# Logits from 64-row products in neighbouring PSUM banks, and wide gate and up products, in a four-layer decoder trunk

## The chip, the cores and the metric

The kernel runs on one core of a Trainium2 chip. The metric is the device time of one execution in microseconds (us). Before the change the median of three runs is 1354.68 us (1350.62 to 1355.57).

## What is computed

Four decoder layers over 256 positions of width 1024, all in float32. A layer is a token mixer, a cross-attention of four heads into 256 memory tokens, one output projection, and a SwiGLU feed-forward block; each of the two sub-layers ends in `x = LayerNorm(alpha * x + sublayer(x))`. Layers 0 and 3 select 64 keys for every query with an indexer and attend to them, layer 1 is a dilated attention of three groups, layer 2 attends causally. All have heads of 64 columns.

```
logits = einsum('bhqd,bhkd->bhqk', q, k) * 64 ** -0.5
p      = softmax(where(mask, logits, -inf))
mix    = einsum('bhqk,bhkd->bhqd', p, v)
x = layer_norm(ALPHA * x + concat(mix, memory_attention) @ w_out)
g, u = split(x @ w_gate_up, 2)            # 1024 -> 2 x 2816
x = layer_norm(ALPHA * x + (silu(g) * u) @ w_down)
```

## The kernel before, in words

**Two parts.** TensorE (PE) multiplies in the type float32r, which keeps fewer bits than float32, so each operand is held in two parts: a high part (`wh`, `xh`, `fth`, `pbh`, ...), a cast that ScalarE (ACT) makes, and a low part (`wl`, `xl`, ...), the difference, which VectorE (DVE) or GpSimd (POOL) makes. `mm3` (L253) is one product in three: high by high, and the two mixed ones (L256 to L258).

**Weights.** They arrive as 128x1024 float32 halves through the SP queue into four `raw` buffers, are cast into one of six pairs of buffers (L214 on ACT, L230 on DVE or L228 on POOL), and are freed by the product that reads them last.

**Products.** `t_mode` (L291) makes a transposed result: for each of two column groups and each of eight 128-row pieces it issues one `mm3` with the weights standing and 256 columns of x moving, and both groups lie in one PSUM bank. The feed-forward block makes 22 such gate and up pieces per layer, the first two in another mode; each is finished by `t_task` (L1055): SiLU on ACT out of PSUM (L1057), a product with the up half on DVE (L1059), a cast (L1061) and a difference (L1063). `down` (L306) uses them with 512 moving columns.

**Mixers.** For a pair of heads, `a_mode` makes q and k for 128 positions in a bank, `rotated` (L462) copies them out (L465), rotates them on DVE (L457 to L460), and transposes them on PE into another bank (L473). `qk_task` (L582) writes q and k from there: `q_parts` puts the high part of a head in one half of the partitions and the low part in the other, `k_parts` and `k_cross` (two more ACT copies, L492 and L493) put each head's k in both halves, so that `logits` (L495) needs one 128-row product per head for 128 keys (L500) and two for 256 keys (L504). `softmax` works in the bank of the logits; `turned` (L548) transposes the probabilities into another bank (L555), from which `split` makes the two parts `pah`/`pal` (128 keys) or `pbh`/`pbl` (256 keys): all casts on ACT (L265), then all differences on DVE (L270). `attend` (L562) multiplies them by the values, and `diag_out` splits the result into `fth`/`ftl`, 64 rows at a time.

**Order.** PE runs in the order in which the Python code issues its instructions. Attention tasks are generators that go on by one step at every `tick`, between pieces of products; a task that finds no free buffer waits a tick. The other engines' order is made from priorities, and each engine works through its own in order.

**Banks.** The eight PSUM banks are a `Slots` list (L86): `pop` takes the bank that was given back longest ago, `put` appends. A bank is given back when its last reader is issued, not when it has run; the next product into that bank waits for the reader. The feed-forward block keeps four banks as accumulators.

```
    def put(self, x):
        self.free.append(x)

    def pop(self):
        return self.free.pop(0)
```

Of the kernel before, what the change touches and what calls it, by code (L numbers as in the profile page):

```python
# [18 lines left out]
S = 256  # L19
# [63 lines left out]
    return out  # L83


class Slots:  # L86
    def __init__(self, items):
        self.free = list(items)
# [24 lines left out]
class K:  # L113
    def __init__(self, tc, io, ctx):
        self.tc, self.nc, self.io = tc, tc.nc, io
        pool = lambda n: ctx.enter_context(tc.tile_pool(name=n, bufs=1))
        self.sb = pool("sb")
        self.pp = ctx.enter_context(tc.tile_pool(name="ps", bufs=1, space=bass.MemoryType.PSUM))

        ctx.enter_context(tc.manual_schedule(engines={mybir.EngineType.PE}))  # L120
        self.stalls = {}
        self.tasks = []
        T = self.t
        pair = lambda shp, tag, n: Slots([(T(shp, F32R, f"{tag}h{i}"), T(shp, F32R, f"{tag}l{i}")) for i in range(n)])
        one = lambda shp, tag, n, dt=F32: Slots([T(shp, dt, f"{tag}{i}") for i in range(n)])
        self.banks = Slots([self.pp.tile([128, 512], F32, name=f"bank{i}") for i in range(8)])
        self.raws = one([128, HALF], "raw", NR)
        self.cvs = pair([128, HALF], "w", NB)
        self.nats = one([128, 256], "nat", 3)
        self.qs = one([128, 2, 128], "q", 4, F32R)  # L130
        self.qms = one([128, 2, S], "qm", 2, F32R)
        self.es = {128: one([128, 2, 128], "e", 3), 256: one([128, 2, 256], "E", 3)}
        self.pTs = {1: pair([128, 1, 2, 128], "pa", 2), 2: pair([128, 2, 2, 128], "pb", 2)}
        self.vs = pair([128, 2, 256], "v", 3)
        self.fts = pair([128, S], "ft", 8)
        self.sils = one([128, S], "sil", 3)
        self.kks = one([128, 2, 2, S], "k", NKB, F32R)
# [3 lines left out]
        self.mk = [T([128, 2, 2, S], F32R, f"mk{i}") for i in range(2)]  # L141
# [149 lines left out]
    def t_mode(self, xT, key):  # L291
        b = self.take(self.banks, "bank")
        p = b.rearrange("p (c t) -> p c t", c=2)
        for c in range(2):
            for k in range(8):
                w = self.half(key, k // 4)
                cs = slice((k % 4) * 256 + c * 128, (k % 4) * 256 + c * 128 + 128)
                self.mm3(p[:, c], (w[0][:, cs], w[1][:, cs]), (xT[0][:, k], xT[1][:, k]), k == 0, k == 7)
                if k % 4 == 3:
                    if c:  # L300
                        self.free_half(key, k // 4)
                    if not (c and k == 7):
                        self.tick()
        return b, p

    def down(self, accs, what, l, kb, tb, ft, first):  # L306
        ts = slice(tb * 128, tb * 128 + 128)
# [168 lines left out]

    def q_parts(self, dst, src, scale=None):

        lo, hi = slice(0, 64), slice(64, 128)
        return [(dst[lo, 0], dst[hi, 0], src[lo], scale), (dst[hi, 1], dst[lo, 1], src[hi], scale)]

    def k_parts(self, dst, src):

        d = dst.rearrange("p h a t -> p a h t")
        n = src.shape[1]
        return d[:, 0], d[:, 1], src[:, None, :].to_broadcast([128, 2, n]), None

    def k_cross(self, dst):  # L490
        lo, hi = slice(0, 64), slice(64, 128)
# [3 lines left out]
    def logits(self, b, q, ks, nk):  # L495

        mm = self.nc.tensor.matmul
        for h in range(2):
            if nk == 128:
                mm(b[:, h * 256:h * 256 + 256].rearrange("p (a s) -> p a s", a=2), lhsT=q[:, h], rhs=ks[h][:, :, 0:128],  # L500
                   start=True, stop=True)
            else:
                for part in range(2):
                    mm(b[:, h * 256:h * 256 + 256], lhsT=q[:, h], rhs=ks[h][:, part], start=part == 0, stop=part == 1)  # L504

    def pair_logits(self, b, q, kb, nk):
        self.logits(b, q, [kb[:, h] for h in range(2)], nk)

    def read_logits(self, b, nk):
        if nk == 128:  # L510
            L = b.rearrange("p (h a s) -> p h a s", h=2, a=2)
            return L[:, :, 0], L[:, :, 1]
        return (b.rearrange("p (h s) -> p h s", h=2),)

    def exps(self, L, e, mn, sm, mask=None, dst=None):

# [14 lines left out]
    def softmax(self, nk, product, mask=None):  # L531

        nc = self.nc
        b = yield from self.tk(self.banks)
        st = yield from self.tk(self.sts)
        e = yield from self.tk(self.es[nk])
        product(b)
        L = self.read_logits(b, nk)
        self.exps(L, e, st[:, 0:2], st[:, 2:4], mask)
        yield W_EXP  # L540
        nc.vector.reciprocal(st[:, 4:6], st[:, 2:4])
        nc.vector.tensor_tensor(e, L[0], st[:, 4:6, None].to_broadcast([128, 2, nk]), op=OP.mult)
        self.banks.put(b)
        self.sts.put(st)
        yield W_NORM
        return e
# [45 lines left out]
    def head_task(self, bank, tb, kb, q, flags, masks, vs, vi, col, mix, kbi):  # L592
# [3 lines left out]
        nk = 128 * (tb + 1)  # L596

        def product(b):
            self.pair_logits(b, q[tb], kb, nk)
# [24 lines left out]

    def mk_piece(self, l):
        b, p = self.t_mode(self.memT, ("mk", l, 0))
        self.split(*(self.k_parts(self.mk[pp], p[:, pp]) for pp in range(2)))
        for pp in range(2):
            self.k_cross(self.mk[pp])
        self.banks.put(b)  # L630
        self.tick()

# [7 lines left out]
    def qm_piece(self, l):  # L640
        b, p = self.t_mode(self.xT, ("qm", l, 0))
        qm = [self.take(self.qms, "qm") for _ in range(2)]
        self.split(*(x for pp in range(2) for x in self.q_parts(qm[pp], p[:, pp], SCALE)))
        self.banks.put(b)
        self.tick()
        return qm
# [1 line left out]
    def mem_task(self, qm, pp, tb, mix):  # L648
        ts = slice(tb * 128, tb * 128 + 128)

        def product(b):
            self.pair_logits(b, qm[pp][:, :, ts], self.mk[pp], S)
# [12 lines left out]
    def ki_task(self, bank, tb, kb, wi, kg, kbb, flags):  # L665
# [21 lines left out]
        self.split((kb[:, 0, 0, tb * 128:tb * 128 + 128], kb[:, 0, 1, tb * 128:tb * 128 + 128], b[:, 0:128], None))  # L687
        self.banks.put(b)
        yield W_K
        flags.add(("k", tb))  # L690
# [1 line left out]
    def qi_task(self, bank, tb, c, qi, mix):  # L692
        b, p = yield from self.rotated(bank, tb)
        for i in range(2):
            qi[tb, 2 * c + i] = mix[2 + 2 * c + i][tb].rearrange("p (h t) -> p h t", h=2)
        self.split(*(x for i in range(2) for x in self.q_parts(qi[tb, 2 * c + i], p[:, i])))
        self.banks.put(b)
        yield W_K
        qi[tb, "ready", c] = True
# [1 line left out]
    def select_task(self, tb, qi, kb, wi, flags, masks):  # L701
# [6 lines left out]
        for pr in range(4):  # L708
            while (tb, "ready", pr // 2) not in qi:
                yield 1  # L710
            b = yield from self.tk(self.banks)
            rl = yield from self.tk(self.es[nk])
            self.logits(b, qi[tb, pr], [kb[:, 0]] * 2, nk)
            L = self.read_logits(b, nk)
            r = L[0]
            if len(L) == 2:
# [148 lines left out]
    def dil_task(self, bank, tb, kb, q, flags, g, parts, jp):  # L865
# [8 lines left out]
        b = yield from self.tk(self.banks)  # L874
        e = yield from self.tk(self.es[nk])
        self.pair_logits(b, q[tb], kb, nk)
        self.qs.put(q[tb])
        flags.add(("l", tb))
        if ("l", 0) in flags and ("l", 1) in flags:
# [155 lines left out]
    def ffn(self, l, ts):  # L1035
# [38 lines left out]
        self.ln_params("ln2", l)  # L1074

        def gu(i):
            b, p = self.t_mode(self.xT, ("gu", l, i))
            fts[i] = self.take(self.fts, "ft")
            gut[i, 0] = gut[i, 1] = self.spawn(t_task(i, b, p))
            self.tick()  # L1080

        def ready(kb, tb):
# [118 lines left out]
```

## Time and profile before

| | |
|---|---|
| median of three runs | 1354.68 us (1350.62 to 1355.57) |
| the profiled execution's own time | 1351.82 us |
| its span | 1350.0 us |
| PE busy | 1287.3 us (95%) |
| PE weight loads busy | 1212.5 us (90%) |
| DVE, ACT, POOL busy | 897.5, 762.9, 316.4 us (66, 57, 23%) |
| granted TensorE clock, mean | 0.983 |
| DMA | 225.65 MB, 167 GB/s over the span |

The span is that of the instructions; the time also holds what lies around them. Matmuls are pipelined: a row's mean duration is longer than the distance between the starts of two that follow each other, and the distance is what a product costs a busy PE. Idle time of an engine that is not the bottleneck costs nothing.

### The profile page before, as it was taken

How to read it: one execution, taken by the hardware profiler on the slowest of the kernel's cores; microseconds unless marked ns; L12 is line 12 of the kernel's file. 1: busy time of each engine (PE TensorE's matmuls, PEld its weight loads, DVE VectorE, ACT ScalarE, POOL GpSimd, SP SyncE). 2: the span in 40 equal slices, each digit the busy share in tenths (PEclk: the TensorE clock that was granted, in tenths of full speed). 3: DMA queues.
4: the chain of work that ended last, by engine and by line, in shares of the span. 5: the costliest groups of instructions: out<-in, count | busy, mean ns of one | idle time of the engine just before them, and what ended most of it. 6: DMA issues, size and time to landing. Idle time of an engine off the chain costs nothing. (4 is left out here: it accounts for less than half of the span.)

```text
span 1350.0 us, 24249 instructions
## 1 busy us (share of the span) xinstructions
PE 1287.3 (95%) x9186; PEld 1212.5 (90%) x9186; DVE 897.5 (66%) x1940; ACT 762.9 (57%) x1512; POOL 316.4 (23%) x277
## 2 busy tenths in 40 slices
PE   6889899999999789999999999999999899999997
PEld 5879799999999779999989989999999898899996
DVE  7887775555578886555567877555568997655555
ACT  5668754444469745444447986444445897544441
POOL 3434440000045343000034444000014533300000
PEclk9989999999999889999999999999999999999999
DMA  8443356556564136565545345666546333655551
GB/s 300 126 149 110 110 180 199 187 188 184 170 203 150 70 103 240 185 189 180 183 155 180 133 141 169 206 185 188 186 138 218 127 125 126 203 188 188 187 176 59
DMA packets 63190, 225.65 MB, mean 167 GB/s; under 512 B 7776, under 2 KB 7776, under 8 KB 63072
## 3 DMA queue, kind: packets, MB, share of 16 engines
q1 hardware_dynamic: 62784, 224.10, 50.2%
q8 instruction: 72, 1.18, 0.4%
q14 instruction: 46, 0.38, 0.1%
q10 hardware_dynamic: 288, 0.00, 0.0%
HBM read 223.02 MB, written 1.05 MB: 166 GB/s over the span
## 5 line engine op out<-in xcount | busy, mean ns | idle before, releaser
L214 ACT CAST wh<-raw 128x1024 fp32r<-128x1024 f32 (+1 forms) x402 | 420.8, 1048 | 318.6 <-PE bank L257 177.2
L230 DVE TENSOR_TENSOR wl<-raw,wh 128x1024 fp32r<-128x1024 f32 (+1 forms) x294 | 378.2, 1288 | 273.9 <-ACT wh L214 269.1
L228 POOL TENSOR_TENSOR wl<-raw,wh 128x512 fp32r<-128x512 f32 x216 | 296.7, 1399 | 727.7 <-ACT wh L214 718.2
L256 PE MATMUL bank<-xh,wh 128*128 128x256 f32 x1344 | 382.1, 284 | 0.0
L257 PE MATMUL bank<-xl,wh 128*128 128x256 f32 x1344 | 381.2, 284 | 0.0
L258 PE MATMUL bank<-xh,wl 128*128 128x256 f32 x1344 | 381.2, 284 | 0.0
L257 PEld LDWEIGHTS bank<-xl,wh 128*128 128x128 f32 x1344 | 258.6, 192 | 1.2
L256 PEld LDWEIGHTS bank<-xh,wh 128*128 128x128 f32 x1344 | 258.6, 192 | 1.3
L258 PEld LDWEIGHTS bank<-xh,wl 128*128 128x128 f32 x1344 | 258.5, 192 | 0.0
L256 PE MATMUL bank<-wh,xh 128*128 128x256 f32 (+1 forms) x768 | 228.5, 298 | 2.8 <-ACT wh L214 1.9
L257 PE MATMUL bank<-wl,xh 128*128 128x256 f32 (+1 forms) x768 | 221.6, 289 | 2.5 <-DVE wl L230 2.3
L258 PE MATMUL bank<-wh,xl 128*128 128x256 f32 (+1 forms) x768 | 221.7, 289 | 0.8 <-DVE xl L270 0.6
L256 PE MATMUL bank<-wh,fth 128*128 128x512 f32 x480 | 189.8, 395 | 0.4 <-ACT fth L265 0.4
L257 PE MATMUL bank<-wl,fth 128*128 128x512 f32 x480 | 188.2, 392 | 0.0
L258 PE MATMUL bank<-wh,ftl 128*128 128x512 f32 x480 | 188.0, 392 | 0.0
L256 PEld LDWEIGHTS bank<-wh,xh 128*128 128x128 f32 x768 | 150.1, 196 | 4.0 <-ACT wh L214 2.4
L257 PEld LDWEIGHTS bank<-wl,xh 128*128 128x128 f32 x768 | 150.1, 195 | 3.1 <-DVE wl L230 3.1
L258 PEld LDWEIGHTS bank<-wh,xl 128*128 128x128 f32 x768 | 149.9, 195 | 1.7 <-DVE xl L270 1.7
L258 PEld LDWEIGHTS bank<-wh,ftl 128*128 128x128 f32 x480 | 90.5, 189 | 19.9 <-DVE ftl L270 0.7
L256 PEld LDWEIGHTS bank<-wh,fth 128*128 128x128 f32 x480 | 90.7, 189 | 17.5 <-ACT fth L265 0.8
L257 PEld LDWEIGHTS bank<-wl,fth 128*128 128x128 f32 x480 | 90.7, 189 | 16.3
L1061 ACT CAST fth<-sil 128x256 fp32r<-128x256 f32 x80 | 32.5, 406 | 107.3 <-DVE sil L1059 107.3
(194 smaller groups left out, 1553.0 us busy)
## 6 DMA issues: line engine op xcount, KB each, us to landing
raw<-in_w SPq DMA_DIRECT2D x396, 512.0 KB, 3.9
lng<-in_ln_g SPq DMA_DIRECT2D x8, 512.0 KB, 4.0
lnb<-in_ln_b SPq DMA_DIRECT2D x8, 512.0 KB, 6.2
raw<-in_w SPq DMA_DIRECT2D x4, 492.0 KB, 4.8
x<-in_xT SPq DMA_DIRECT2D x2, 512.0 KB, 5.4
E<-in_mem SPq DMA_DIRECT2D x4, 256.0 KB, 5.6
x<-in_x SPq DMA_DIRECT2D x2, 512.0 KB, 6.0
out_x<-x SPq DMA_DIRECT2D x4, 256.0 KB, 2.2
```

The source lines that it names most:

```text
L214: self.nc.scalar.copy(c[0][:, 0:wd], self.raw[n][:, 0:wd])
L228: self.nc.gpsimd.tensor_tensor(lo[:, c], r[:, c], hi[:, c], op=OP.subtract)
L230: self.nc.vector.tensor_tensor(lo[:, 0:wd], r[:, 0:wd], hi[:, 0:wd], op=OP.subtract)
L256: mm(out, lhsT=ah, rhs=bh, start=first, stop=False)
L257: mm(out, lhsT=ah, rhs=bl, start=False, stop=False)
L258: mm(out, lhsT=al, rhs=bh, start=False, stop=last)
L1061: nc.scalar.copy(fts[i][0], s)
```

## The change

Four things change.

1. **Banks.** The eight banks become one PSUM tile. `Banks.pop` takes first a free bank whose neighbour (numbers 0 and 1, 2 and 3, ...) is not free; `pop2` takes two neighbours.
2. **Logits.** q and k are kept as they come out of the transposes, in a high and a low part over all 128 partitions. Each head's logits are products of 64 rows, head 0 on partitions 0 to 63, head 1 on 64 to 127, in turn, into the two banks of a pair: for 256 keys six products of 256 columns, for 128 keys two of 256 and two of 128. `q_parts`, `k_parts` and `k_cross` go.
3. **x.** Its two parts lie side by side in one tile, so that 512 columns hold both parts of a piece.
4. **Gate and up.** `wide_mode` takes the place of `t_mode` in 20 of the 22 pieces of each layer: per column group four products of the high weights with 512 columns, then four of the low weights with 256. The two column groups lie in two banks; `t_task` copies the second half of each bank out (ACT), adds the first half to it (DVE), and goes on from there.

```diff
+class Banks:
+
+    def __init__(self, tile):
+        self.tile, self.free = tile, list(range(8))
+
+    def pop(self, why=None):
+        lone = [i for i in self.free if i ^ 1 not in self.free]
+        i = (lone or self.free)[0]
+        self.free.remove(i)
+        return self.tile[:, i]
+
+    def pair(self):
+        return next((i for i in self.free if not i % 2 and i + 1 in self.free or i % 2 and i - 1 in self.free), None)
+
+    def pop2(self):
+        i = self.pair() & ~1
+        self.free.remove(i)
+        self.free.remove(i + 1)
+        return self.tile[:, i:i + 2]
+
+    def put(self, x):
+        first, n = (x.offset // 512) % 8, x.shape[1] if len(x.shape) == 3 else 1
+        self.free += range(first, first + n)
...
-        self.banks = Slots([self.pp.tile([128, 512], F32, name=f"bank{i}") for i in range(8)])
+        self.banks = Banks(self.pp.tile([128, 8, 512], F32, name="bank"))
...
-        self.xT = (T([128, 8, S], F32R, "xh"), T([128, 8, S], F32R, "xl"))
+        self.x2 = T([128, 8, 2, S], F32R, "x2")
+        self.xT = (self.x2[:, :, 0], self.x2[:, :, 1])
...
+    def wide_mode(self, key):
+
+
+        mm = self.nc.tensor.matmul
+        bs = [self.take(self.banks, "bank") for _ in range(2)]
+        for c in range(2):
+            for h in range(2):
+                w = self.half(key, h)
+                cs = [slice(k * 256 + c * 128, k * 256 + c * 128 + 128) for k in range(4)]
+                for k in range(4):
+                    mm(bs[c], lhsT=w[0][:, cs[k]], rhs=self.x2[:, 4 * h + k].rearrange("p a t -> p (a t)"),
+                       start=h == k == 0, stop=False)
+                for k in range(4):
+                    mm(bs[c][:, 0:S], lhsT=w[1][:, cs[k]], rhs=self.x2[:, 4 * h + k, 0], start=False, stop=h == 1 and k == 3)
...
-    def k_cross(self, dst):
-        lo, hi = slice(0, 64), slice(64, 128)
-        self.nc.scalar.copy(dst[hi, 0], dst[lo, 0])
-        self.nc.scalar.copy(dst[lo, 1], dst[hi, 1])
...
+    def logits(self, bs, q, k, nk):
+
+
         mm = self.nc.tensor.matmul
...
+        rows = [slice(0, 64), slice(64, 128)]
         if nk == 128:
...
+            for h, r in enumerate(rows):
+                mm(bs[:, h, 0:256].rearrange("p (a s) -> p a s", a=2), lhsT=q[r, 0], rhs=k[r, :, 0:128], start=True, stop=False)
+            for h, r in enumerate(rows):
+                mm(bs[:, h, 0:128], lhsT=q[r, 1], rhs=k[r, 0, 0:128], start=False, stop=True)
+            return
+        for n, (a, c) in enumerate(((0, 0), (0, 1), (1, 0))):
+            for h, r in enumerate(rows):
+                mm(bs[:, h, 0:256], lhsT=q[r, a], rhs=k[r, c], start=n == 0, stop=n == 2)
...
     def softmax(self, nk, product, mask=None):
 
         nc = self.nc
-        b = yield from self.tk(self.banks)
         st = yield from self.tk(self.sts)
         e = yield from self.tk(self.es[nk])
+        b = yield from self.tk2()
         product(b)
...
-        k = kb[:, :, :, tb * 128:tb * 128 + 128]
-        self.split(self.k_parts(k, p[:, 1]), *self.q_parts(q[tb], p[:, 0], SCALE))
-        self.k_cross(k)
+        k = kb[:, :, tb * 128:tb * 128 + 128]
+        self.split(self.parts_of(k, p[:, 1]), self.parts_of(q[tb], p[:, 0], SCALE))
...
-        def t_task(i, b, p):
+        def t_task(i, bs):
             s = yield from self.tk(self.sils)
-            nc.scalar.activation(s, p[:, 0], AF.Silu)
+            u = yield from self.tk(self.sils)
+            for d, b in ((s, bs[0]), (u, bs[1])):
+                nc.scalar.copy(d, b[:, S:2 * S])
+                nc.vector.tensor_tensor(d, b[:, 0:S], d, op=OP.add)
+                self.banks.put(b)
+            nc.scalar.activation(s, s, AF.Silu)
             yield 1
-            nc.vector.tensor_tensor(s, s, p[:, 1], op=OP.mult)
-            self.banks.put(b)
+            nc.vector.tensor_tensor(s, s, u, op=OP.mult)
+            self.sils.put(u)
             nc.scalar.copy(fts[i][0], s)
```

The first place is on PE in the mixer of layer 2, where a task ends its `attend`, the next one transposes its probabilities, and a third its q and k. The numbers before the arrow are the buffers: before, each bank is a tile of its own (`bank6`, `bank2`, `bank3`, `bank4`).

```order
L258 MATMUL bank4_67<-wh1_77,xl_151 128x256
L256 MATMUL bank6_69<-pbh0_106,vh1_112 128x256 [waits Activation_49]
L257 MATMUL bank6_69<-pbl0_107,vh1_112 128x256 [waits DVE_49]
L258 MATMUL bank6_69<-pbh0_106,vl1_113 128x256
L256 MATMUL bank6_69<-pbh0_106,vh1_112 128x256
L257 MATMUL bank6_69<-pbl0_107,vh1_112 128x256
L258 MATMUL bank6_69<-pbh0_106,vl1_113 128x256
L555 MATMUL bank2_65<-ident_226,e0_96 128x128 x2
L473 MATMUL bank3_66<-ident_226,nat0_87 128x128 x2
L256 MATMUL bank4_67<-wh2_79,xh_150 128x256
```

With the change the same instructions stand in the same order at this place (L282 to L284 are the three lines of `mm3`, L592 is L555, L519 is L473), all in the one tile `bank`.

```order
L284 MATMUL bank_63<-wh1_70,x2_143 128x256
L282 MATMUL bank_63<-pbh0_99,vh1_105 128x256 [waits Activation_49]
L283 MATMUL bank_63<-pbl0_100,vh1_105 128x256 [waits DVE_49]
L284 MATMUL bank_63<-pbh0_99,vl1_106 128x256
L282 MATMUL bank_63<-pbh0_99,vh1_105 128x256
L283 MATMUL bank_63<-pbl0_100,vh1_105 128x256
L284 MATMUL bank_63<-pbh0_99,vl1_106 128x256
L592 MATMUL bank_63<-ident_218,e0_89 128x128 [waits DVE_49]
L592 MATMUL bank_63<-ident_218,e0_89 128x128
L519 MATMUL bank_63<-ident_218,nat0_80 128x128 [waits DVE_49]
L519 MATMUL bank_63<-ident_218,nat0_80 128x128
L282 MATMUL bank_63<-wh2_72,x2_143 128x256
```

What is new is that both transposes wait for DVE. `pop` gives all three steps the same bank, number 5: the products of `attend` go into it, its reader is issued and it is given back; its neighbour is in use, so it is the first that `pop` takes for the transposes of `e0`, and, given back again, for those of `nat0`.

The second place is on PE in the feed-forward block: one gate and up piece (names as above, L342 and L345 are the two products of `wide_mode`).

```order
L284 MATMUL bank_63<-wh4_76,ftl7_124 128x512
L342 MATMUL bank_63<-x2_143,wh5_78 128x512 x4
L345 MATMUL bank_63<-x2_143,wl5_79 128x256 x4
L342 MATMUL bank_63<-x2_143,wh0_68 128x512 x4
L345 MATMUL bank_63<-x2_143,wl0_69 128x256 x4
L342 MATMUL bank_63<-x2_143,wh5_78 128x512 x4
L345 MATMUL bank_63<-x2_143,wl5_79 128x256 x4
L342 MATMUL bank_63<-x2_143,wh0_68 128x512 x4
L345 MATMUL bank_63<-x2_143,wl0_69 128x256 x4
```

Before, 48 products of 256 columns stood here, sixteen times L256, L257, L258; now 16 of 512 and 16 of 256. The products around the piece have not moved.

## Rows read from the trace of the kernel before

**Rows 1.** Busy us by stage: mixers (1st, 3rd, 4th, 5th row), feed-forward (2nd); columns first

```profile
core 0: us, PE busy (x) PEld busy (x) DVE busy (x) ACT busy (x) POOL busy (x), PEclk, DMA share, GB/s
0.00:188.00 188.00, 160.14 (x1107) 149.11 (x1108) 149.92 (x455) 126.09 (x301) 81.03 (x95) 0.94 0.46 158
188.00:388.00 200.00, 199.92 (x1434) 189.21 (x1433) 113.00 (x142) 94.28 (x132) 20.72 (x15) 1.00 0.58 188
388.00:500.00 112.00, 98.93 (x696) 93.01 (x695) 88.09 (x260) 76.19 (x206) 46.20 (x34) 0.92 0.38 128
...
707.00:815.00 108.00, 102.91 (x766) 96.59 (x765) 84.41 (x257) 85.78 (x227) 47.86 (x38) 1.00 0.43 143
...
1021.00:1150.00 129.00, 122.09 (x909) 115.35 (x908) 113.62 (x387) 102.10 (x266) 56.33 (x49) 1.00 0.42 140
```

**Rows 2.** Timeline, feed-forward of layer 0, PE: start us, duration us

```profile
219.90 0.28 PE L256 MATMUL bank<-xh,wh 128*128 128x256 f32 x1
...
222.06 0.40 PE L256 MATMUL bank<-wh,fth 128*128 128x512 f32 x1
...
227.53 0.28 PE L256 MATMUL bank<-xh,wh 128*128 128x256 f32 x1
```

**Rows 3.** Groups by line: count, busy us, mean ns of one; end of a piece

```profile
L1059 DVE TENSOR_TENSOR sil<-sil,bank 128x256 f32<-128x256 f32 x80 | 33.1, 414 | 0.0
...
L1061 ACT CAST fth<-sil 128x256 fp32r<-128x256 f32 x80 | 32.5, 406 | 107.3 <-DVE sil L1059 107.3
```

**Rows 4.** Groups by line: readers of PSUM banks in the mixers

```profile
L265 ACT CAST fth<-bank 64x128 fp32r<-64x128 f32 x128 | 33.0, 258 | 17.5 <-PE bank L258 15.9 <-DVE nat L460 0.6
...
L270 DVE TENSOR_TENSOR ftl<-bank,fth 64x128 fp32r<-64x128 f32 x112 | 32.1, 287 | 25.1 <-ACT fth L265 23.0 <-PE bank L473 0.6
...
L270 DVE TENSOR_TENSOR pbl<-bank,pbh 128x512 fp32r<-128x512 f32 x36 | 24.8, 688 | 2.8 <-ACT pbh L265 1.8
...
L265 ACT CAST pbh<-bank 128x512 fp32r<-128x512 f32 x36 | 21.0, 583 | 4.2 <-PE bank L555 3.6
...
L270 DVE TENSOR_TENSOR pal<-bank,pah 128x256 fp32r<-128x256 f32 x20 | 8.4, 421 | 3.5 <-ACT pah L265 3.3
...
L265 ACT CAST pah<-bank 128x256 fp32r<-128x256 f32 x20 | 7.4, 371 | 3.4 <-PE bank L555 3.1
```

**Rows 5.** Timeline, mixer of layer 2, all engines, at 786.8 us

```profile
786.82 0.29 PE L258 MATMUL bank<-pah,vl 128*128 128x256 f32 x1
786.82 1.05 ACT L214 CAST wh<-raw 128x1024 fp32r<-128x1024 f32 x1 [0.26 <-issue]
...
786.94 0.60 PE L555 MATMUL bank<-ident,E 128*128 128x128 f32 x4
...
787.38 0.38 PE L473 MATMUL bank<-ident,nat 128*128 128x128 f32 x2
...
788.33 0.59 DVE L270 TENSOR_TENSOR ftl<-bank,fth 64x128 fp32r<-64x128 f32 x2 [1.41 <-ACT fth L265]
...
788.96 0.69 DVE L270 TENSOR_TENSOR pbl<-bank,pbh 128x512 fp32r<-128x512 f32 x1
```

**Rows 6.** Groups by line: the logits

```profile
L504 PE MATMUL bank<-k,q 128*128 128x256 f32 x96 | 17.9, 307 | 4.8 <-ACT E L529 2.5 <-ACT k L492 2.3
...
L500 PE MATMUL bank<-k,q 128*128 128x256 f32 x48 | 11.1, 308 | 2.2 <-ACT k L492 2.0
...
L504 PE MATMUL bank<-mk,qm 128*128 128x256 f32 x64 | 10.5, 286 | 0.0
...
L504 PE MATMUL bank<-k,ftl 128*128 128x256 f32 x32 | 5.7, 304 | 0.0
...
L500 PE MATMUL bank<-k,fth 128*128 128x256 f32 x16 | 3.7, 314 | 0.0
```

**Rows 7.** Timeline of PE, mixer of layer 0: a wait, in brackets

```profile
68.93 1.01 PE L500 MATMUL bank<-k,q 128*128 128x256 f32 x2 [2.04 <-ACT k L492]
```

**Rows 8.** Busy us by stretch, mixer of layer 0; columns as in Rows 1

```profile
69.30:72.50 3.20, 3.17 (x14) 2.85 (x13) 3.14 (x17) 0.81 (x3) 1.37 (x3) 0.53 0.40 116
```

More of the change, by code (lines that the diff above doesn't have):

```diff
@@ L136, in __init__ @@
         self.sils = one([128, S], "sil", 3)
-        self.kks = one([128, 2, 2, S], "k", NKB, F32R)
+        self.kks = one([128, 2, S], "k", NKB, F32R)
         self.sts = one([128, 64], "st", 12)
-        self.xT = (T([128, 8, S], F32R, "xh"), T([128, 8, S], F32R, "xl"))
+        self.x2 = T([128, 8, 2, S], F32R, "x2")
+        self.xT = (self.x2[:, :, 0], self.x2[:, :, 1])
         self.memT = (T([128, 8, S], F32R, "mh"), T([128, 8, S], F32R, "ml"))
-        self.mk = [T([128, 2, 2, S], F32R, f"mk{i}") for i in range(2)]
+        self.mk = [T([128, 2, S], F32R, f"mk{i}") for i in range(2)]
         self.mv = (T([128, 2, 256], F32R, "mvh"), T([128, 2, 256], F32R, "mvl"))
@@ L304, in t_mode @@
         return b, p
+    def wide_mode(self, key):
[10 more added lines that the diff above has]
+                    mm(bs[c][:, 0:S], lhsT=w[1][:, cs[k]], rhs=self.x2[:, 4 * h + k, 0], start=False, stop=h == 1 and k == 3)
+                if c:
+                    self.free_half(key, h)
+                if not (c and h):
+                    self.tick()
+        return bs
     def down(self, accs, what, l, kb, tb, ft, first):
@@ L475, in rotated @@
         return b, p
-    def q_parts(self, dst, src, scale=None):
-        lo, hi = slice(0, 64), slice(64, 128)
[L482 to L488, printed above, removed]
-    def k_cross(self, dst):
-        lo, hi = slice(0, 64), slice(64, 128)
-        self.nc.scalar.copy(dst[hi, 0], dst[lo, 0])
-        self.nc.scalar.copy(dst[lo, 1], dst[hi, 1])
@@ L495, in logits @@
-    def logits(self, b, q, ks, nk):
-        mm = self.nc.tensor.matmul
[L498 to L507, printed above, removed]
@@ L509, in read_logits, with parts_of, tk2 @@
-    def read_logits(self, b, nk):
-        if nk == 128:
-            L = b.rearrange("p (h a s) -> p h a s", h=2, a=2)
-            return L[:, :, 0], L[:, :, 1]
-        return (b.rearrange("p (h s) -> p h s", h=2),)
+    def parts_of(self, dst, src, scale=None):
+        return dst[:, 0], dst[:, 1], src, scale
+    def tk2(self):
+        while self.banks.pair() is None:
+            yield 1
+        return self.banks.pop2()
+    def logits(self, bs, q, k, nk):
+        mm = self.nc.tensor.matmul
+        rows = [slice(0, 64), slice(64, 128)]
+        if nk == 128:
+            for h, r in enumerate(rows):
[6 more added lines that the diff above has]
+                mm(bs[:, h, 0:256], lhsT=q[r, a], rhs=k[r, c], start=n == 0, stop=n == 2)
@@ L515, in exps, with read_logits @@
+    def read_logits(self, bs, nk):
+        return [bs[:, :, c:c + nk] for c in range(0, 256, nk)]
     def exps(self, L, e, mn, sm, mask=None, dst=None):
@@ L598, in product @@
         def product(b):
-            self.pair_logits(b, q[tb], kb, nk)
+            self.logits(b, q[tb], kb, nk)
             self.qs.put(q[tb])
@@ L626, in mk_piece @@
         b, p = self.t_mode(self.memT, ("mk", l, 0))
-        self.split(*(self.k_parts(self.mk[pp], p[:, pp]) for pp in range(2)))
-        for pp in range(2):
-            self.k_cross(self.mk[pp])
+        self.split(*(self.parts_of(self.mk[pp], p[:, pp]) for pp in range(2)))
         self.banks.put(b)
@@ L642, in qm_piece @@
         qm = [self.take(self.qms, "qm") for _ in range(2)]
-        self.split(*(x for pp in range(2) for x in self.q_parts(qm[pp], p[:, pp], SCALE)))
+        self.split(*(self.parts_of(qm[pp], p[:, pp], SCALE) for pp in range(2)))
         self.banks.put(b)
@@ L651, in product @@
         def product(b):
-            self.pair_logits(b, qm[pp][:, :, ts], self.mk[pp], S)
+            self.logits(b, qm[pp][:, :, ts], self.mk[pp], S)
         e = yield from self.softmax(S, product)
@@ L686, in ki_task @@
         nc.tensor.transpose(b[:, 0:128], kd, self.ident)
-        self.split((kb[:, 0, 0, tb * 128:tb * 128 + 128], kb[:, 0, 1, tb * 128:tb * 128 + 128], b[:, 0:128], None))
+        self.split(self.parts_of(kb[:, :, tb * 128:tb * 128 + 128], b[:, 0:128]))
         self.banks.put(b)
@@ L695, in qi_task @@
             qi[tb, 2 * c + i] = mix[2 + 2 * c + i][tb].rearrange("p (h t) -> p h t", h=2)
-        self.split(*(x for i in range(2) for x in self.q_parts(qi[tb, 2 * c + i], p[:, i])))
+        self.split(*(self.parts_of(qi[tb, 2 * c + i], p[:, i]) for i in range(2)))
         self.banks.put(b)
@@ L710, in select_task @@
                 yield 1
-            b = yield from self.tk(self.banks)
             rl = yield from self.tk(self.es[nk])
-            self.logits(b, qi[tb, pr], [kb[:, 0]] * 2, nk)
+            b = yield from self.tk2()
+            self.logits(b, qi[tb, pr], kb, nk)
             L = self.read_logits(b, nk)
@@ L873, in dil_task @@
         st = parts[jp, tb, "st"]
-        b = yield from self.tk(self.banks)
         e = yield from self.tk(self.es[nk])
-        self.pair_logits(b, q[tb], kb, nk)
+        b = yield from self.tk2()
+        self.logits(b, q[tb], kb, nk)
         self.qs.put(q[tb])
@@ L1076, in gu @@
         def gu(i):
-            b, p = self.t_mode(self.xT, ("gu", l, i))
+            bs = self.wide_mode(("gu", l, i))
             fts[i] = self.take(self.fts, "ft")
-            gut[i, 0] = gut[i, 1] = self.spawn(t_task(i, b, p))
+            gut[i, 0] = gut[i, 1] = self.spawn(t_task(i, bs))
             self.tick()
```

## The prediction

> **What bounds the kernel now.** I read the table of stages first. In the feed-forward block PE is busy for 199.92 of 200 us, with DVE at 113 and ACT at 94 [rows 1]: there only the number and the spacing of PE's products count, and work on ACT and DVE is free as long as it fits. In the four mixers PE is idle for 28, 13, 5 and 7 us, 53 in all [rows 1]: long chains across PE, ACT and DVE, which PE mostly covers by going on with other pieces. Then the timeline of a feed-forward stretch gives the spacing: 18 products of 256 columns start within 2.16 us, 0.120 each, and 24 of 512 within 5.47, 0.228 each [rows 2]. Twice the columns cost less than twice the time. Last, for the mixers, a stretch of the timeline and the groups that read PSUM banks [rows 4, 5].
>
> **Gate and up.** 80 pieces (20 per layer), each of 16 triples of 256 columns, become 16 pairs of 512 and 256: 0.228 + 0.120 = 0.348 instead of 0.360, 0.012 less, times 1280: **-15.4 us**. PE is saturated there, so it shows in full. The price is two more ACT copies and two more DVE additions per piece, about as long as the piece's other steps, 0.41 [rows 3]: 20 pieces add 16 us to ACT's 94 and 17 to DVE's 113, under a PE time of nearly 200. A piece's banks are taken again two pieces later, and its result is used at least one piece later (48 products of 0.12, 5.8 us), while its chain grows by about 1.6 us. Cost nothing; if PE were not the bound there, the gain would go.
>
> **Banks.** This is the large term. A product into a bank waits until the bank's last reader has run. Before, `pop` took the bank that had been free longest, so the reader had long ended. Now it prefers a bank whose neighbour is in use, and the bank just given back usually is one. In the first order shown ahead, `attend`, the transposes of `e0` and those of `nat0` follow each other in bank 5, and each must wait until ACT and DVE have emptied it. I followed pops and puts through the whole changed program and counted the writes whose bank's reader needs PE work less than 0.3 us ahead (so that PE has nothing to do meanwhile): **55 places, none in the feed-forward block** (17, 6, 16 and 16 by layer), against 2 before, both behind `k_cross`. Readers: 20 times `ftl` (after `attend`), 17 `pbl`, 8 `pal`, 10 others. Another 23 places have 0.3 to 1.5 us of cover, before 10.
>
> What one costs, at least: the product's own 0.29, the casts, the difference, less the spacing that was there anyway. `ftl`: 0.29 + 2 x 0.258 + 0.287 - 0.12 = 0.97; `pbl`: 0.29 + 0.583 + 0.688 - 0.11 = 1.45; `pal`: 0.29 + 0.371 + 0.421 - 0.11 = 0.97 [rows 4]; the ten others taken as 0.97. Sum: 20 x 0.97 + 17 x 1.45 + 18 x 0.97 = 61.5, or 1.12 each. At most, as one such place runs before, where PE does not wait: the product of `attend` starts at 786.82 and its `ftl` ends at 788.92, the transposes start at 786.94 and their `pbl` ends at 789.65, while PE went on at 787.38 in another bank [rows 5]. That is 2.10 and 2.71 where the floors are 1.09 and 1.56: a weight cast of 1.05 lay ahead on ACT. With such a cast everywhere it would be 55 x 2.2 = 120. I take the floor and 0.4: ACT is busy two thirds of a mixer [rows 1], and while PE waits no new weight buffers come free for it to cast. 55 x 1.52 = **+83**, bounds 61 and 120. The 13 new places with some cover: 0.4 each, **+5**.
>
> **Waits that go.** `k_cross` is gone, and with it PE's waits for L492, 2.3 and 2.0 us [rows 6]. Of the other 49 idle us in the mixers some are waits for attention results that now come ready while PE stands at a bank; a quarter, 12. **-16**, bounds -4 and -30.
>
> **Logits.** 48 calls for 256 keys had four products, 32 calls for 128 keys two (192 and 64 products [rows 6]). Now they have six, and two of 256 with two of 128 columns. If both heads' products run side by side, three spacings replace four: 48 x -0.12 = -5.8, and nothing for 128 keys (0.12 + 0.11, by the transposes, four of which take 0.44 [rows 5], for 0.24). If they run one after the other: 48 x 0.24 + 32 x 0.22 = +18.6. No row shows a 64-row product, so I take the middle: **+6**.
>
> The Trainium skill speaks against this edit: "TensorEngine Tiling (Array Packing)", Key Properties, says that different tiles run in parallel but that a change of the tiling mode drains the engine. The first half would give the low end; the second is a rival below. No run here shows either yet.
>
> **Clock.** After the wait of 2.04 us [rows 7] PE had a granted clock of 0.53 for 3.2 us [rows 8], mostly its lower level of 1.2 GHz; such a stretch loses 1.5 us. The mixers of layers 0 and 1 are at 0.94 and 0.92, those of layers 2 and 3, with little idle time, at 1.00 [rows 1]. Places where two waits follow each other closely will look like that wait: about ten, 10 x 1.5 = **+14** rounded down, bounds 0 and 30.
>
> The skill's "TensorE: Matmul & The Clock Gate", section "A second HAM failure mode: psum-queue depth-cycling", describes a kernel that paused often between groups of products while cycling through PSUM banks, and whose clock swung between the levels. By it this term lies nearer its upper bound; by the rows of layers 2 and 3, nearer zero.
>
> **Sum.** -15.4 + 83 + 5 - 16 + 6 + 14 = +76.6. The profiled execution took 1351.8, 0.2% under the median of the runs: 1351.8 + 76.6 = **1428 us**. All the low ends together: -15.4 + 61 + 2 - 30 - 6 + 0 = +12, 1364. All the high ends: -15.4 + 120 + 9 - 4 + 19 + 30 = +159, 1510.
>
> **Rivals.**
> *Cheap waits* (0.10): the waits stand at their floor, and PE's standstill lets the other chains catch up, so that the mixers' old waits go: near the low ends, 1360 to 1385. For it: ACT and DVE are a third idle. Against: the place above.
> *Faster* (0.05): the waits cost PE almost nothing, and what remains is -15.4 - 4.3 - 5.8, 1326. It would need readers that end before PE comes; with the 5 us above, a mean wait under (25.5 - 5)/55 = 0.37 us decides for it, under half of the lowest floor. That a 512-column product did not save its 0.012 would only take this gain away, 15 us on any case.
> *Drain* (0.08): each of the 80 calls changes the mode twice and empties PE. A product lasts 0.28 where its spacing is 0.12 [rows 2], so a drain costs about 0.16: 160 x 0.16 = 26, with products in a row (18.6): 39 above my 6, 1467. It comes on top of the bank waits.
> *Between* (0.04): the terms cancel within 0.5%, if the mean wait is about 0.4 us. Only a mixture gives it.
> The forecast, bank waits that decide, 1385 to 1455: 0.73.
>
> **Numbers.** About 0.5% (6.8 us) is what a measurement can tell here. Slower: 0.73 + 0.10 + 0.08 = 0.91; faster 0.05; same 0.04. The range from 1370 to 1480 takes in the forecast, the drain and most of the cheap waits, and leaves out about 0.15.
>
> **What would show it.** Right: in the four mixers PE waits for DVE's `ftl`, `pbl` and `pal` from L296 (the difference in `split`) at L592 (transposes in `turned`), L519 (those in `rotated`) and the logits' lines, some 55 times for 1 to 2 us, and PE's idle time there grows from 53 to some 130 us; in the feed-forward block the spacing is 0.228 and 0.120 and a stage is some 4 us shorter; no L492. Wrong: PE runs through these places, or its idle time lies at the weights or in the feed-forward block (DVE or ACT become the bound there), or the logits' rows show pairs more than 0.3 us apart.

## The result, and the profile after

The changed kernel takes 1473.3 us (median of four runs, 1464.9 to 1475.6) where the kernel before, run beside it, takes 1354.2 (1350.6 to 1355.6): ratio 1.087, 95% interval 1.082 to 1.092, 119 us slower. The forecast was 1428 with a range of 1370 to 1480. The profiled execution of the change was the shortest of the four, 1464.9, with a span of 1463.1; the other three had a mean granted clock of 0.96 against its 0.97. What follows splits this span against that of before, 1350.0: +113.

First the table of stages, cut at the same points of the program as [rows 1]: mixers are the 1st, 3rd, 5th and 7th row, feed-forward blocks the others.

```profile
core 0: us, PE busy (x) PEld busy (x) DVE busy (x) ACT busy (x) POOL busy (x), PEclk, DMA share, GB/s
0.00:216.00 216.00, 168.56 (x1148) 149.41 (x1149) 139.34 (x433) 105.57 (x250) 77.29 (x94) 0.93 0.40 137
216.00:414.00 198.00, 196.18 (x1104) 171.04 (x1102) 129.16 (x181) 104.19 (x168) 21.51 (x16) 1.00 0.58 190
414.00:532.00 118.00, 101.70 (x740) 92.12 (x741) 77.80 (x247) 62.06 (x169) 46.99 (x34) 0.99 0.34 122
532.00:737.00 205.00, 202.61 (x1141) 176.77 (x1140) 135.95 (x194) 108.73 (x171) 26.68 (x20) 1.00 0.56 188
737.00:881.00 144.00, 115.38 (x814) 102.67 (x813) 78.26 (x241) 71.22 (x187) 47.88 (x37) 0.96 0.32 107
881.00:1085.00 204.00, 201.51 (x1135) 175.72 (x1134) 134.49 (x191) 107.06 (x171) 25.91 (x20) 1.00 0.57 187
1085.00:1266.00 181.00, 146.39 (x973) 131.20 (x972) 111.11 (x367) 86.95 (x222) 56.57 (x48) 0.90 0.30 100
```

The mixers have grown from 188, 112, 108 and 129 us [rows 1] to 216, 118, 144 and 181. PE's idle time in them is 47 + 16 + 29 + 35 = 127 us, before 53. A feed-forward block is only some 2 us shorter. DVE and ACT are less busy in the mixers than before: the loss is standstill, not work.

Then PE's own waits. Columns: us in total, number, longest.

```profile
PE bank L592 <- DVE ftl L296: 23.8, 15, 2.6
PE bank L546 <- DVE pbl L296: 11.8, 7, 3.3
PE bank L519 <- DVE pbl L296: 10.8, 8, 2.0
PE bank L368 <- DVE x L296: 8.9, 8, 1.8
PE bank L519 <- DVE nat L506: 7.7, 2, 5.1
PE bank L519 <- DVE bank L504: 6.1, 1, 6.1
PE bank L519 <- DVE ftl L296: 5.8, 6, 1.2
...
PE bank L519 <- DVE pal L296: 4.4, 4, 1.5
```

These are the readers that were named: `ftl`, `pbl`, `pal`, at the transposes and at the logits. No row names the copies of `k_cross` (L492 before) any more. One row was not foreseen: L368, the transposes of x at a layer's end, eight times.

How such a wait runs is seen at the place of [rows 5], where before PE went on in other banks:

```profile
846.75 0.29 DVE L296 TENSOR_TENSOR ftl<-bank,fth 64x128 fp32r<-64x128 f32 x1
847.11 0.66 PE L592 MATMUL bank<-ident,E 128*128 128x128 f32 x4 [1.88 <-DVE ftl L296]
847.80 0.58 ACT L291 CAST pbh<-bank 128x512 fp32r<-128x512 f32 x1 [1.37 <-PE bank L592]
848.42 0.69 DVE L296 TENSOR_TENSOR pbl<-bank,pbh 128x512 fp32r<-128x512 f32 x1 [1.37 <-ACT pbh L291]
...
849.16 0.44 PE L519 MATMUL bank<-ident,nat 128*128 128x128 f32 x2 [1.40 <-DVE pbl L296]
```

PE, ACT and DVE take turns, and each of the three shows idle time in brackets: PE 1.88 until `ftl` has left the bank, ACT and DVE 1.37 until PE and ACT have delivered, PE 1.40 again. Nothing covers anything.

The feed-forward block, timeline of PE:

```profile
324.02 1.09 PE L342 MATMUL bank<-x,wh 128*128 128x512 f32 x4
324.95 0.63 PE L345 MATMUL bank<-x,wl 128*128 128x256 f32 x4
325.43 1.09 PE L342 MATMUL bank<-x,wh 128*128 128x512 f32 x4
```

Four pairs take 1.41 here; over the block the mean is 0.351 a pair, against 0.348 forecast and 0.360 before. And a logits call for 256 keys, with the 128-row products beside it:

```profile
455.24 0.28 PE L284 MATMUL bank<-pbh,mvl 128*128 128x256 f32 x1
455.45 0.62 PE L546 MATMUL bank<-mk,qm 64*128 64x256 f32 x6
456.00 0.39 PE L282 MATMUL bank<-wh,x 128*128 128x256 f32 x1
456.22 0.28 PE L283 MATMUL bank<-wl,x 128*128 128x256 f32 x1
```

Six products in 0.55 us: they run two at a time. But the distance into the call is 0.21 and the one behind the first product after it 0.22, where 0.12 is usual. From 455.24 to 456.22 are 0.98 us; the four 128-row products of before took six distances of 0.12 here, 0.72.

**Where the span went.** I set the distance between the starts of every two products that follow each other against the usual spacing of their columns [rows 2] (a 64-row product counts half). What is more than 0.25 us above it I call a wait; what the lower clock adds to the usual spacing stands by itself, and so does the short excess around 64-row calls. "Tight" is the number of places where the bank's reader has less than 0.3 us of PE work as cover, counted in the program. The columns e1 to e9 are experiments, told in the next section.

| us | before | change | e1 | e2 | e3 | e4 | e9 |
|---|---|---|---|---|---|---|---|
| usual spacing | 1234.4 | 1209.9 | 1234.4 | 1217.4 | 1209.9 | 1226.9 | 1209.9 |
| waits (number) | 61.6 (46) | 156.3 (105) | 213.0 (113) | 60.5 (50) | 68.9 (58) | 154.3 (104) | 75.6 (65) |
| lower clock | 15.6 | 30.6 | 71.8 | 19.0 | 16.0 | 37.8 | 15.3 |
| edges of 64-row calls | 0 | 27.2 | 0 | 0 | 27.8 | 27.4 | 28.6 |
| tight places | 2 | 55 | 69 | 2 | 15 | 55 | 8 |

The count hangs a little on what is taken as the reader's start. Counted on the programs as built, from the last product that wrote the bank, it is 0, 56, 64, 0, 7, 56 and 8, with waits of 0, 98, 141, 0, 11, 98 and 13 us. What is said below of the change, e1, e4 and e9 holds by either count; for e3 only the order of size does.

Change against before: -24.5 + 94.7 + 15.0 + 27.2, and 0.7 of small rests: +113.

### The profile page after: what moved, and what is told of

Its sections match the earlier page's. It is cut to its first block, busy times and chain, and to the rows that moved or that the text cites. A ratio compares the mean times of both kernels' runs of the same rounds, so it can differ in the third digit from the quotient of the medians.

```text
span 1463.1 us, 22194 instructions
## 1 busy us (share of the span) xinstructions
PE 1319.7 (90%) x8066; PEld 1160.2 (79%) x8066; DVE 932.1 (64%) x2028; ACT 740.1 (51%) x1488; POOL 314.8 (22%) x277
## 3 DMA queue, kind: packets, MB, share of 16 engines
q8 instruction: 63, 1.03, 0.3%
## 5 line engine op out<-in xcount | busy, mean ns | idle before, releaser
L256 DVE TENSOR_TENSOR wl<-raw,wh 128x1024 fp32r<-128x1024 f32 (+1 forms) x294 | 377.7, 1294 | 182.4 <-ACT wh L240 142.1
L342 PE MATMUL bank<-x,wh 128*128 128x512 f32 x1280 | 349.3, 394 | 0.0
L342 PEld LDWEIGHTS bank<-x,wh 128*128 128x128 f32 x1280 | 221.0, 189 | 31.3
L282 PE MATMUL bank<-wh,x 128*128 128x256 f32 (+1 forms) x768 | 239.4, 312 | 6.7 <-ACT wh L240 2.1
L283 PE MATMUL bank<-wl,x 128*128 128x256 f32 (+1 forms) x768 | 227.5, 296 | 2.1 <-DVE wl L256 2.1
L284 PE MATMUL bank<-wh,x 128*128 128x256 f32 (+1 forms) x768 | 227.5, 296 | 0.7 <-DVE x L296 0.7
L345 PEld LDWEIGHTS bank<-x,wl 128*128 128x128 f32 x1280 | 196.2, 189 | 27.0
L345 PE MATMUL bank<-x,wl 128*128 128x256 f32 x1280 | 203.4, 281 | 0.0
L282 PE MATMUL bank<-wh,fth 128*128 128x512 f32 x480 | 189.6, 395 | 0.4 <-ACT fth L291 0.4
L284 PE MATMUL bank<-wh,ftl 128*128 128x512 f32 x480 | 188.0, 392 | 0.0
L282 PEld LDWEIGHTS bank<-wh,x 128*128 128x128 f32 x768 | 155.6, 203 | 13.2 <-ACT wh L240 2.8
L283 PEld LDWEIGHTS bank<-wl,x 128*128 128x128 f32 x768 | 156.3, 203 | 2.6 <-DVE wl L256 2.6
L284 PEld LDWEIGHTS bank<-wh,x 128*128 128x128 f32 x768 | 156.0, 203 | 1.1 <-DVE x L296 1.1
L284 PEld LDWEIGHTS bank<-wh,ftl 128*128 128x128 f32 x480 | 90.1, 188 | 20.0 <-DVE ftl L296 0.7
L282 PEld LDWEIGHTS bank<-wh,fth 128*128 128x128 f32 x480 | 90.3, 188 | 18.8 <-ACT fth L291 0.9
L1093 ACT COPY sil<-bank 128x256 f32<-128x256 f32 x160 | 58.5, 366 | 61.4 <-PE bank L345 61.4
L1094 DVE TENSOR_TENSOR sil<-bank,sil 128x256 f32<-128x256 f32 x160 | 67.1, 419 | 30.7 <-ACT sil L1093 30.7
```

The lines of the kernel that those rows point to most:

```text
L256: self.nc.vector.tensor_tensor(lo[:, 0:wd], r[:, 0:wd], hi[:, 0:wd], op=OP.subtract)
L282: mm(out, lhsT=ah, rhs=bh, start=first, stop=False)
L283: mm(out, lhsT=ah, rhs=bl, start=False, stop=False)
L284: mm(out, lhsT=al, rhs=bh, start=False, stop=last)
L342: mm(bs[c], lhsT=w[0][:, cs[k]], rhs=self.x2[:, 4 * h + k].rearrange("p a t -> p (a t)"), start=h == k == 0, stop=False)
L345: mm(bs[c][:, 0:S], lhsT=w[1][:, cs[k]], rhs=self.x2[:, 4 * h + k, 0], start=False, stop=h == 1 and k == 3)
```

## The experiments

Three theories stood against each other: banks taken again too soon (the forecast), the 64-row logits with their change of shape (a rival), the longer chain of a gate and up piece (the cover that the prediction set at nothing).

**e1: the bank rule alone.** The kernel before, with the change's `pop`:

```diff
-        self.banks = Slots([self.pp.tile([128, 512], F32, name=f"bank{i}") for i in range(8)])
+        self.banks = Banks(self.pp.tile([128, 8, 512], F32, name="bank"))
```

> The kernel before with one edit: a bank is taken as in the change (first a free bank whose neighbour is in use); 128-row logits, gate and up, x and q, k as before. Theory (banks taken again too soon are the loss): this alone is slower than the kernel before by at least as much as the whole change. Following pops and puts there are 69 places where PE comes to a bank less than 0.3 us of PE work after its reader could start, against 55 with the change and 2 before. In the trace of the change the 55 cost 97 us, 1.76 each; 69 x 1.76 = 121, some 25 for places with more cover and 15 for the clock, less some 25 of old waits: about 1490, between 1455 and 1520. Rival (the 64-row logits are the loss, by switching PE between tile shapes): within 10 us of 1354, as it has no 64-row product. Rival (wide gate and up): the same, about 1354.

Measured: 1557.6 us, ratio 1.152 (1.149 to 1.154). One rule for handing out banks, with no 64-row product and no wide piece, costs 205 us, more than the whole change; both rivals fall as the main cause. The edit also lays the eight banks into one tile; e3 keeps that tile and loses the waits, so it is not the tile. The size was missed: the 69 places cost 149.5 us, 2.17 each instead of 1.76, and the lower clock 56 us more than before instead of 15. Waits of PE, and the first 208 us, which lie within the first mixer:

```profile
PE bank L580 <- DVE ftl L295: 26.9, 14, 2.8
PE bank L529 <- DVE ftl L295: 13.9, 8, 2.4
PE bank L281 <- DVE nat L485: 10.4, 6, 2.3
```

```profile
0.00:208.00 208.00, 146.83 (x912) 134.29 (x913) 128.82 (x408) 110.43 (x269) 62.26 (x81) 0.84 0.35 124
```

L580 and L529 are the transposes and the logits, as L592 and L546 above; the readers are the same kind. PE's granted clock over these 208 us is 0.84, before 0.94 over the first 188 [rows 1]. The Trainium skill's "TensorE: Matmul & The Clock Gate", section "A second HAM failure mode: psum-queue depth-cycling", tells of a kernel whose short pauses between groups of products, while it cycles through PSUM banks, made the clock swing: e1 agrees (56 us), the change itself only in part (15).

**e2: wide gate and up alone.** `wide_mode`, x in one tile and the new `t_task` put into the kernel before:

```diff
-            b, p = self.t_mode(self.xT, ("gu", l, i))
+            bs = self.wide_mode(("gu", l, i))
```

> The kernel before with the wide gate and up alone (x's two parts in one tile, products of 512 and 256 columns, the new tail); banks in the old order, old logits. Theory: in the trace of the change a feed-forward stage is 2 to 2.7 us shorter, with pairs 0.351 apart instead of 0.348 forecast and 0.360 before: 1280 x 0.009 = 11, about 1343, between 1339 and 1347. My prediction's own figure: 1339. Rival (the longer chain of a piece, two copies and two additions more, makes ACT or DVE late in the feed-forward block): 1354 or more.

Measured: 1343.1 us, ratio 0.993 (0.991 to 0.995), as expected. The waits are those of before (60.5 against 61.6): the longer chain is covered, as predicted. This part is a gain by itself, and e2 is the version that beats both kernels.

**e3: the change with the banks in turn.**

```diff
-        lone = [i for i in self.free if i ^ 1 not in self.free]
-        i = (lone or self.free)[0]
-        self.free.remove(i)
-        return self.tile[:, i]
+        return self.tile[:, self.free.pop(0)]
...
-        return next((i for i in self.free if not i % 2 and i + 1 in self.free or i % 2 and i - 1 in self.free), None)
+        whole = [i for i in self.free if i ^ 1 in self.free]
+        return min(whole, key=lambda i: max(self.free.index(i), self.free.index(i ^ 1)), default=None)
```

> The change with one edit: a single bank is again the one given back longest ago, and of the free pairs the one that is complete longest; everything else as in the change. 15 tight places are left of 55, and 27 with 0.3 to 1.6 us of cover of 49. Theory (banks): 40 x 1.76 = 70 us go, some 15 of the others, some 12 of the clock's; perhaps 20 of the old waits come back: 1473 - 97 + 20 = about 1395, between 1370 and 1415. Rival (64-row logits): at least 1455, since these are untouched.

Measured: 1364.2 us, ratio 1.009 (1.007 to 1.011): 109 of the 119 us go by this edit, and the rival (at least 1455) falls. I had expected 1395, with 20 us of old waits come back; the waits are 68.9 us in all, where my figures made some 90 (156 - 70 - 15 + 20). What is left above before is the 64-row logits with the pairs of banks that they need: e3 differs from e2 in these, and the table gives -7.5 of spacing, +27.8 of edges, +8.4 of waits, -3.0 of clock and some -5 of small rests: +21. The mixers of layers 0 and 3, cut near the points of the table of stages:

```profile
0.00:193.00 193.00, 166.25 (x1157) 149.34 (x1158) 140.47 (x434) 105.51 (x253) 80.05 (x95) 0.94 0.45 155
1021.00:1163.00 142.00, 130.13 (x955) 117.02 (x954) 107.91 (x365) 84.46 (x220) 55.61 (x48) 0.99 0.38 127
```

They last 193 and 142 us with PE idle for 27 and 12; in the change it was 216 and 181, with 47 and 35 idle.

**e4: the change without wide gate and up** (the edit of e2 the other way round).

> The change without its wide gate and up (256-column triples and their tail as before), with the banks' policy and the 64-row logits of the change. Theory: the feed-forward gain is lost and nothing else moves, the count of tight places is the same 55: 1473 + 11 = 1484, between 1478 and 1490. Rival (the wide pieces' longer chain costs in the mixers or in the feed-forward block): 1473 or less.

Measured: 1482.3 us, ratio 1.094 (1.090 to 1.099), as expected. The 55 tight places cost 96.9 us, in the change 97.0: the wide pieces have no part in them.

**e5 and e6: what a change of shape costs.** Into the 80 wide pieces of e2 goes one product more, in e5 with all 128 rows, in e6 with 64. It adds work whose result is written over.

```diff
+                if not c and not h:
+                    for _ in range(1):
+                        mm(bs[1][:, 0:S], lhsT=w[0][0:64, cs[0]], rhs=self.x2[0:64, 0, 0], start=True, stop=True)
```

> The kernel of e2 (wide gate and up alone, 1343.1) with one more product in each of the 80 wide pieces: 256 columns, all 128 rows, into the piece's second bank, which is written anew afterwards. It is the control for e6 and lies in the feed-forward block, where PE waits for nothing. Both theories: 80 x 0.12 = 9.6, about 1353.

> As e5, but the extra product has 64 rows (the first half of the same operands). Theory (each change between 128-row and 64-row products empties PE): around the 64-row calls in the trace of the change the four distances (into the call, to the second pair, out of it, to the product behind) are 0.21, 0.22, 0.21 and 0.22 instead of 0.12, some 0.37 more per call; 80 x (0.12 + 0.37) = 39, about 1382, between 1372 and 1388. Rival (the longer distances belong to the logits, to their banks or to operands just written, and not to the change of shape): as e5, 1353.

Measured: e5 1350.7 us, ratio 0.999 (0.998 to 1.000), 7.6 above e2 where 9.6 was expected; e6 1380.5, ratio 1.021 (1.020 to 1.023). The difference is 29.7 us, 0.37 per piece. Timeline of PE in e5, the extra product at L323:

```profile
219.24 0.28 PE L323 MATMUL bank<-x,wh 128*128 128x256 f32 x1
219.36 1.09 PE L317 MATMUL bank<-x,wh 128*128 128x512 f32 x4
220.29 0.63 PE L320 MATMUL bank<-x,wl 128*128 128x256 f32 x4
```

and in e6:

```profile
220.37 0.38 PE L323 MATMUL bank<-x,wh 64*128 64x256 f32 x1
220.68 1.19 PE L317 MATMUL bank<-x,wh 128*128 128x512 f32 x4
221.71 0.63 PE L320 MATMUL bank<-x,wl 128*128 128x256 f32 x4
```

From the extra product to the next L317 are 0.12 and 0.31, and the four L317 take 0.93 and 1.03; the way into the extra product is 0.09 longer too (0.209 against 0.120, means of 16 and 17 places between 200 and 340 us). So the excess comes with one product of another shape, without any logits, and at a place where PE waits for nothing else. Key Properties in the Trainium skill's "TensorEngine Tiling (Array Packing)" says that a change of the tiling mode drains the engine: e6 agrees, 0.37 there and back. That different tiles work in parallel, the other half of that passage, the 0.55 us of a call bear out too.

**e7: 512 and 256 columns in turn** in e2's pieces.

```diff
                 for k in range(4):
                     mm(bs[c], lhsT=w[0][:, cs[k]], rhs=self.x2[:, 4 * h + k].rearrange("p a t -> p (a t)"),
                        start=h == k == 0, stop=False)
-                for k in range(4):
                     mm(bs[c][:, 0:S], lhsT=w[1][:, cs[k]], rhs=self.x2[:, 4 * h + k, 0], start=False, stop=h == 1 and k == 3)
```

> The kernel of e2 with the products of a wide piece in another order: 512 and 256 columns in turn, row piece by row piece, instead of four and then four. In the trace of the change 512 behind 512 comes after 0.232 to 0.234, 256 behind 512 after 0.229, 256 behind 256 after 0.118, 512 behind 256 after 0.119. Theory (the order decides which of these distances occur): 0.348 a pair instead of 0.351, 1280 x 0.003 = 4 us, about 1339, distances seen in the trace. Rival (four in a row are as good or better): 1343 or more.

Measured: 1345.3 us, ratio 0.995 (0.993 to 0.997), the same as e2. My expectation was wrong: 256 behind 512 now comes after 0.236, 512 behind 256 after 0.117, 0.353 a pair. The distances do not hang on the pattern alone.

**e8: head after head** in e3's logits, instead of the heads in turn.

```diff
-        for n, (a, c) in enumerate(((0, 0), (0, 1), (1, 0))):
-            for h, r in enumerate(rows):
+        for h, r in enumerate(rows):
...
+            for n, (a, c) in enumerate(((0, 0), (0, 1), (1, 0))):
                 mm(bs[:, h, 0:256], lhsT=q[r, a], rhs=k[r, c], start=n == 0, stop=n == 2)
```

> The kernel of e3 (the change with banks in turn, 1364.2) with the logits' products of head 0 first and then those of head 1, instead of the heads in turn. Theory (the two heads run side by side only when they stand next to each other in PE's order): for 256 keys five or six distances of 0.12 instead of three, for 128 keys three or four instead of two: 48 x 0.24 + 32 x 0.12 = 15 to twice that, 1379 to 1394. Rival (the order within a call does not matter, or they don't run side by side at all): 1364.

Measured: 1366.5 us, ratio 1.011 (1.009 to 1.013), 2 us from e3: the rival. Timeline of PE:

```profile
407.44 0.28 PE L282 MATMUL bank<-wh,x 128*128 128x256 f32 x1
407.65 0.62 PE L542 MATMUL bank<-k,q 64*128 64x256 f32 x6
408.20 0.39 PE L280 MATMUL bank<-wh,x 128*128 128x256 f32 x1
408.42 0.28 PE L281 MATMUL bank<-wl,x 128*128 128x256 f32 x1
```

The call takes 0.55, exactly as with the heads in turn, and the six starts within it come in pairs 0.01 apart. That a pair is one product of each head is seen in a call for 128 keys, where each head has first a product of 256 columns (L538) and then one of 128 (L539):

```profile
474.78 0.39 PE L538 MATMUL bank<-k,q 64*128 64x256 f32 x2
475.00 0.23 PE L539 MATMUL bank<-k,q 64*128 64x128 f32 x2
```

Both L538 start together, though in PE's order the L539 of head 0 stands between them. So products of head 1 that stand behind those of head 0 still run beside them.

**e9: never the newest bank.** The change's preference for a bank with a neighbour in use stays; only the one given back last is left out (and of the pairs the oldest is taken, as in e3).

```diff
-        lone = [i for i in self.free if i ^ 1 not in self.free]
-        i = (lone or self.free)[0]
+        old = self.free[:max(1, len(self.free) - 1)]
+        lone = [i for i in old if i ^ 1 not in self.free]
+        i = (lone or old)[0]
```

> The change with another edit of its bank rule: a bank with a neighbour in use is still preferred, but never the one given back last (unless it is the only one); of the free pairs the one that is complete longest. By the count 8 tight places are left (55 in the change, 15 in e3) and 45 with 0.3 to 1.6 us of cover (49 and 27). Theory (how lately the bank was read decides, not the preference for a lone bank): the tight ones 8 x 1.5 = 12 us, the covered ones as in the change, where 30 of 49 showed a wait of 1.03: 28 us, the rest 30 as in e3, together 70 against 68.9 in e3: about 1365, between 1356 and 1376. Rival (the preference for lone banks is the loss in itself, for example by what it does to the pairs): over 1430.

Measured: 1368.2 us, ratio 1.012 (1.010 to 1.013), as expected. The 8 tight places cost some 13 us; all other waits, some 63, are about as many as the kernel before has in all (61.6). So the preference itself costs little here; that the bank was read a moment ago does.

## Why the prediction was right, and where its sum was short

**Right: the cause and the places.** I laid the program's order beside the trace's products. All 55 places showed a wait of more than 0.25 us, together 97.0 us; before, the two tight places cost 2.4. PE's idle time in the mixers came to 127 us where "some 130" was said. That this fits so closely is partly luck: it has grown by 74 us by busy time and the waits by 94.7 by the starts, since by busy time the first 0.16 of a wait (0.28 less 0.12) counts as busy, and the forecast added up costs by the starts. e1, e3, e4 and e9 show it from four sides: with 69, 15, 55 and 8 tight places the waits are 213, 69, 154 and 76 us. Between e3 and e9 the places with more cover decide.

**Not by the time alone.** 1473 lies inside the range, but above the forecast's own stretch of 1385 to 1455 and next to the 1467 of the drain rival. The time could not tell the two apart; e1 and e3 do. The banks took 109 of the 119 us, and the drain came on top of them.

**Mis-sized: the price of a place.** Forecast 55 x 1.52 = 83, measured 55 x 1.76 = 97. The readers apart: `ftl` 20 times 1.90 (I had 0.97 + 0.4), `pbl` 17 times 1.81 (1.45 + 0.4), `pal` 8 times 1.42 (0.97 + 0.4), the others ten times 1.69. The floor of `ftl` was wrong: I counted one difference where there are two, one for each head; [rows 5] shows them, x2 in 0.59. An undisturbed place in the change:

```profile
98.02 0.53 ACT L291 CAST fth<-bank 64x128 fp32r<-64x128 f32 x2 [1.05 <-PE bank L284]
98.59 0.59 DVE L296 TENSOR_TENSOR ftl<-bank,fth 64x128 fp32r<-64x128 f32 x2 [0.24 <-ACT fth L291]
99.23 0.44 PE L592 MATMUL bank<-ident,e 128*128 128x128 f32 x2 [1.30 <-DVE ftl L296]
```

Two casts, two differences, and some 0.05 at each hand-over; the excess is 1.46. At two places that I looked at, where a weight cast lay directly ahead on ACT (803.49 and 1232.61 us), it was 2.04 and 2.01, near the 2.10 that the upper bound was made of.

**Most wrong: "the 13 new places with some cover", +5.** By the trace, places with 0.3 to 1.6 us of cover cost 30.9 us in 30 waits, before 3.1 in 6: +27.8. I drew the line at 1.5, and 14 of the waits, 17.9 us, have a cover of 1.55: among them the eight transposes of x (10.2 by the starts), and the transposes of `e` behind q's split. And I gave each 0.4 where the 16 waits inside the line cost 0.8 each. (Counted on the programs as built, the term is 26.5 us in 23 waits, before none.) A chain of cast and difference lasts as long as that cover, so a line at 1.5 cut through the middle of them.

**Waits that go: -16, measured -28.** All other waits fell from 56 to 28 us: more than I took, within the bound of -30. That it is PE's standstill that lets the chains catch up is the prediction's reading; no run tests it by itself.

**Logits: +6, measured +19.7.** The spacing gives -7.5, below the low end of -5.8: the heads run side by side. The edges give +27.2, which is the drain rival's figure of 26, without its products in a row. I took the middle between two ends that were both about the spacing, and left the edges to a rival that I joined with the wrong spacing; half of each was true. That the edges alone have this price is shown by e6 (29.7 us for 80 of them).

**Gate and up: -15.4, measured -11.** The spacing of 512 columns is 0.234 between four in a row, not the 0.228 of `down` [rows 2]; nothing else was late (e2).

**Clock: +14, measured +15.** The size is right, the place was not told: the mixer of layer 3 has most of the rise (granted 1.00 before [rows 1], 0.90 now), layer 2's went from 1.00 to 0.96, and layer 1's came up from 0.92 to 0.99. The "about ten" close pairs were not counted in the trace, so this figure may be right by luck.

Together: 97 - 2 + 28 - 28 + 19.7 - 11 + 15 = +118.7, less some 5 of small excess that I did not split further: +113. The forecast had +77. It was short by 34 us on the two terms of the banks, by 14 on the logits and by 4 on gate and up, and over by 12 on the waits that go and by the 5 of small excess. The other 8 us up to the median of 1473 are between the profiled execution, the shortest one, and the others; with their clock of 0.96 they may well lie in the clock's term, but they have no trace.

## What to carry to other kernels

When a pool of PSUM banks is handed out in program order, the age of a bank is its cover: the preference that kept picking the newest one put PE, ACT and DVE in series (e1; e9 mends it), and it can be counted in the program before it runs, place by place, with the readers' full chain (every cast and difference of every head) as the line between covered and not. A change made of several parts is to be timed part by part: here one part gained 10 us (e2), one cost about 20 (e3 against e2), and a few lines of bookkeeping 109. Small tiles have a price for each trip there and back, here 0.37 us against the 0.12 that a call for 256 keys saves. By these figures a call would have to be some three times as long to pay for its trip; this is an estimate that no run tried.

## What was not expected of the hardware

Two 64-row products on different halves of the rows run side by side even if the other two products of the first half stand between them in PE's order (e8, a call of 0.55 us either way).

512 columns with new weights every time cost 0.228 in `down` [rows 2] and 0.234 to 0.236 in the wide pieces (e2, e7); why, stays open. So does why a tight place costs 2.17 in e1 and 1.76 in the change; I did not try it.
